# A decoder layer in split float32: gated products and sums on VectorE, a planner that waits for late work, and attention in four groups

## The chip, the cores and the metric

One core of one Trainium2 chip. The time is that of one execution on the device in microseconds (us). The engines are called as in the profile: PE (TensorE, with PEld for its weight loads), DVE (VectorE), ACT (ScalarE), POOL (GpSimd) and SP (SyncE, which issues most of the loads). Lines (L417) are lines of the kernel before, unless the text says after.

## The reference, cut to what matters

One layer for 256 tokens of width 1024 in float32: a pooling mixer and a causal attention with 8 heads of 64 share an input and an output projection; then cross-attention of 4 heads of 256 into 256 memory tokens; then a gated FFN. Each of the three adds its result to a scaled residual and is followed by a layer norm.

```python
z = h @ w_in[l]
u = z[..., :POOL_WIDTH]
q, k, v = ...            # three slices of z, 8 heads of 64 each
pool_out = multiscale_pool(u, w_pool[l], pool_scale[l])
attn_out = moba_attention(q, k, v)          # 256 tokens: one causal block
mix = jnp.concatenate([pool_out, attn_out], axis=-1) @ w_out[l]
h = layer_norm(DEEPNORM_ALPHA * h + mix, ln1_g[l], ln1_b[l])
h = layer_norm(DEEPNORM_ALPHA * h + memory_cross_attention(h, mem, w_xq[l], w_xkv[l], w_xo[l]), ln2_g[l], ln2_b[l])
h = layer_norm(DEEPNORM_ALPHA * h + (jax.nn.silu(h @ w_gate) * (h @ w_up)) @ w_down, ln3_g[l], ln3_b[l])
```

## The kernel before

**Numbers in two parts.** A float32 value is split into two float32r numbers, a high part (ACT casts: w67h from w67r) and a rest (DVE subtracts: w67l). `split` (L473) records the two. A product of two split values is three matmuls, high by high and the two mixed ones (`three`, L465). Scores, attention outputs of the 8 small heads, and transposes are in plain float32. Weights come as pages of 128 x 1024, numbered in order of use: w0 to w16 for q and k, then v, u (from w21 on the memory projections stand beside them), w27 to w34 w_out, w43 to w50 the query projection of the cross-attention, w51 to w58 w_xo, w59 onwards the FFN.

**Who decides the order.** The program first records all its operations in a `Plan` (L138) and then gives each engine a fixed list. PE works in the order in which the code is written. All other engines get their order from a simulation of the whole run: `deadlines` (L190) gives every operation a time by which PE needs it, and `schedule` (L227) lets each engine take, among the operations that are ready by the plan's clock, the one with the earliest deadline. How long an operation takes there is a formula (`cost`, L384). An engine never stands idle for an operation that is not yet ready, if any other is.

**The stages in time.** Projections to q and k; then `do_v`, `do_u` and `do_xk` (the memory keys), generators that PE works off in steps (the code from L871 on). Between their steps stand the small operations of the attention, `scores(hq, t)` (L738: four heads, one tile of 128 queries), `probs_t(hp)` (L766: transposes of the softmax of a pair of heads), `attend(hp)` (L792), and of the pooling, `mix_pool(g)` (its output is the c blocks, c0l for one). After w_out and the first norm comes the cross-attention: `do_xq(h)` for the query projection, with `xscores` (L1047), `xprobs_t` (L1058: transposes of xpr into xst) and `xattend` (L1067: outputs o0 to o3, split into o3h and o3l) between the steps of it and of `project(c_xo, ...)`. `Norm` (L920) does a norm on DVE: `sum` and `measure` for each half of 512 columns, `stats` (with a power on POOL, L945), `centre` and `scale`. In LN2 r20 and r21 are the two tiles of 128 tokens; PE then transposes them into h2T (`ident,r`), which is split too.

**The FFN.** DFF = 2816 in 11 chunks of 256. The first chunk goes by rows of tokens (`rows_of_first`: seven of its eight k steps for tile 0, 21 matmuls, then the first transposes of tile 1). For each of the other ten, `gated` (L1161) adds the two PSUM parts of gate and up on DVE, applies Silu on ACT, and multiplies the two (128 x 512) on POOL. Chunks 1 to 8 multiply with w_down by a seven-product scheme, for which `add_sums` (L1150) forms four sums of the quarters of the gated values, 128 x 128 each, on POOL; the sums of weight quarters come from DRAM for chunks 1 to 6 and are formed on DVE for 7 and 8 (d7, d8). The down phase follows the last chunk, from about 322 us.

Of the kernel before, what the change touches and what calls it, by code (L numbers as in the profile page):

```python
# [18 lines left out]
P = 128  # L19
D = 1024  # L20
S = 256
# [19 lines left out]
class Buf:  # L41
# [11 lines left out]
    @property  # L53
    def grain(self):
        return 512 if self.kind == "bank" else GRAIN
# [72 lines left out]
class Op:  # L128
    __slots__ = ("n", "eng", "fn", "busy", "late", "preds", "succs", "dead", "ready", "wait", "start", "end",
                 "bufs", "locks", "size", "kind", "bias")  # L130
# [4 lines left out]
LEAVE = 2.0  # L135


class Plan:  # L138
# [88 lines left out]
    def schedule(self, room):  # L227
# [10 lines left out]
        free = {"PE": 0.0, "ACT": 0.0, "DVE": 0.0, "POOL": 0.0, "SP": 0.0, "AQ": 0.0}  # L238
        wire = 0.0
        ready = {e: [] for e in free}  # L240
        for o in self.ops:
            o.wait, o.ready = len(o.preds), 0.0
# [4 lines left out]
        dve_lock = 0.0  # L247
        stall = []
# [48 lines left out]
        while len(done) < total:  # L297
            moved = False
            for e in free:
                if free[e] > t:  # L300
                    continue
# [7 lines left out]
                else:  # L309
                    later, tries = [], 0  # L310
                    while ready[e] and tries < 40:
                        item = heappop(ready[e])
                        c = item[2]
                        if c.ready <= t and place(c, t):
                            o = c
                            break
                        later.append(item)
                        tries += 1
# [32 lines left out]
                for s in o.succs:  # L351
# [5 lines left out]
                    s.ready = max(s.ready, at)  # L357
# [4 lines left out]
            nxt = [a for a in free.values() if a > t]  # L362
# [14 lines left out]
class Kit:  # L377


    def __init__(self, nc, plan):  # L380
        self.nc, self.plan = nc, plan
        self.engines = {"ACT": nc.scalar, "DVE": nc.vector, "POOL": nc.gpsimd, "SP": nc.sync, "AQ": nc.scalar}
# [20 lines left out]
    def act(self, out, src, func, bias=0.0, scale=1.0, accum=None, **kw):  # L403
# [7 lines left out]
        busy, late = self.cost("ACT", out.cols)  # L411
        outs = [out] + ([accum] if accum is not None else [])
# [25 lines left out]
    def dma(self, out, src, size, queue="SP", after=(), bias=0.0):  # L438
        q = self.engines[queue]
        val = lambda v: v.ap() if isinstance(v, View) else v  # L440
        return self.plan.op(queue, lambda: q.dma_start(val(out), val(src)), [out], [src], 0.1 if queue == "SP" else 0.4,
                            3.0 + size / 300e3, size=size, after=after, bias=bias)

    def dma_add(self, out, src, size, after=()):
# [3 lines left out]
                            [out], [src], 1.3, 6.0 + size / 100e3, size=2.5 * size, after=after)  # L448
# [38 lines left out]
def decoder_layer(  # L487
    ctx: ExitStack, tc: tile.TileContext, x, x_t, mem_t, w_qkv, w_u, w_pool, w_out,
    ln1_g, ln1_b, w_xq, w_xk, w_xkv, w_xo, ln2_g, ln2_b, w_gu, w_down, w_sum, ln3_g, ln3_b, out,
# [103 lines left out]
    c_qk[0].cut = {0: [(slice(0, 256), "AQ", [slice(0, 128), slice(128, 256)]), (slice(256, 512), "SP", [slice(256, 512)])]}  # L593
# [61 lines left out]
    for _ in range(BUSY):  # L655
        plan.op("PE", lambda: nc.tensor.matmul(ps.ap()[:, :P], spark, spark, start=True, stop=True), [ps], [], 0.22,
# [56 lines left out]


# [23 lines left out]
    def scores(hq, t):  # L738
        w = (t + 1) * P
        pss = [bank(f"ps{j}").re("p (h s) -> p h s", h=2) for j in range(2)]  # L740
        for h in range(2):
            for j in range(2):
# [3 lines left out]
                   0.007 if j == 0 else 2 * w / 2400)  # L746
# [41 lines left out]

    def block_of(name, k):
        return tuple(a[:, 2 * (k % 2):2 * (k % 2) + 2, :].re("p t s -> p (t s)") for a in pair_of(name, k // 2))  # L790

    def attend(hp):  # L792
        s0, s1 = pts[hp]
        po = bank("po")
        for j in range(2):
            hs = slice(j * HD, (j + 1) * HD)
            vs = slice((2 * hp + j) * HD, (2 * hp + j + 1) * HD)
            mm(po[hs, :S], vt[:, 0, vs], s0[:, j, :], True, False, 0.013 if j == 0 else 0.25)
            mm(po[hs, P:S], vt[:, 1, vs], s1[:, j, :], False, True, 0.013 if j == 0 else 0.1)
        split(*block_of("c", 4 + hp), po[:, :S])  # L800
# [19 lines left out]
    def mix_pool(g):  # L820
# [6 lines left out]
        hi, lo = block_of("c", g)  # L827
        act(hi, pm, AF.Copy, 0.0, psc[:, g:g + 1])
        stt(lo, pm, psc[:, g:g + 1], hi.f32, OP.mult, OP.subtract)
# [54 lines left out]
    run(u, 6)  # L884
    scores(1, 1)
# [6 lines left out]
    run(gk, 12)  # L892
    probs_t(2)
    mix_pool(0)
    run(gk, 8)
    probs_t(3)
    mix_pool(1)
    pool_diff(2)
    run(gk, 8)
    attend(2)  # L900
    mix_pool(2)
    pool_diff(3)
    run(gk, 8)
    attend(3)
    mix_pool(3)
    run(gk)

# [93 lines left out]
    mix = project(c_mix, lambda k: block_of("c", k), 4)  # L1001
    norms = []
    for t in range(T):
        norm = Norm(1, t, xt[t])
        for half_ in HALVES:
            norm.add(*half_, until(mix)[1])
        norm.finish()
        norms.append(norm)
    run(mix)
# [16 lines left out]
    gv = do_xv()
    run(gv, 8)
# [418 lines left out]
```

## Time and profile before

| | |
|---|---|
| median of 3 runs | 385.34 us (384.01 to 385.57) |
| the profiled execution, its own time | 385.47 us |
| its span | 383.7 us |
| PE busy | 371.7 us (97% of the span) |
| DVE busy | 286.6 us (75%) |
| ACT busy | 214.7 us (56%) |
| POOL busy | 66.3 us (17%) |
| HBM traffic over the span | 244 GB/s |

Busy time is the union of an engine's instructions; matmuls are pipelined, and their ends are modelled, so PE's pace is read from start to start. In a timeline a row has the start in us, the duration, the engine, the line, the operation, output and inputs with their shapes; "x4" means that four like instructions stand in one row; the bracket at the end is the idle time ahead of it and the instruction that ended it.

### The profile page before, as it was taken

How to read it: one execution, taken by the hardware profiler on the slowest of the kernel's cores; microseconds unless marked ns; L12 is line 12 of the kernel's file. 1: busy time of each engine (PE TensorE's matmuls, PEld its weight loads, DVE VectorE, ACT ScalarE, POOL GpSimd, SP SyncE). 2: the span in 40 equal slices, each digit the busy share in tenths (PEclk: the TensorE clock that was granted, in tenths of full speed). 3: DMA queues.
4: the chain of work that ended last, by engine and by line, in shares of the span. 5: the costliest groups of instructions: out<-in, count | busy, mean ns of one | idle time of the engine just before them, and what ended most of it. 6: DMA issues, size and time to landing. Idle time of an engine off the chain costs nothing.

```text
span 383.7 us, 5499 instructions
## 1 busy us (share of the span) xinstructions
PE 371.7 (97%) x2058; PEld 317.9 (83%) x2058; DVE 286.6 (75%) x384; ACT 214.7 (56%) x324; POOL 66.3 (17%) x73
## 2 busy tenths in 40 slices
PE   8999999999999999899969999999999999999994
PEld 7997878788888898888848888888888888888883
DVE  5889577966599646576898375373866998999994
ACT  5779778643346527458447144452746867677310
POOL 1000027000010000000100073263346440100012
PEclk9999999999999999999998999999999999999999
DMA  7999436376687534538476999998754465999002
GB/s 245 416 417 417 178 111 182 110 252 170 222 287 261 160 114 143 187 113 290 143 289 205 364 381 274 272 278 214 191 181 141 123 188 141 305 386 343 3 2 109
DMA packets 25690, 84.50 MB, mean 220 GB/s; under 512 B 2752, under 2 KB 3520, under 8 KB 25664
## 3 DMA queue, kind: packets, MB, share of 16 engines
q1 hardware_dynamic: 24544, 79.11, 59.0%
q0 software_dynamic: 832, 4.72, 6.6%
q8 instruction: 16, 0.26, 0.3%
q10 hardware_dynamic: 288, 0.33, 0.2%
q14 instruction: 10, 0.08, 0.1%
HBM read 83.10 MB, written 10.49 MB: 244 GB/s over the span
## 4 chain that ended last, share of the span: by engine, by line
PE 72%; issue 14%; DVE 6%; ACT 3%; DMA 3%; POOL 1%; SPq 0%; POOLq 0%; DVEq 0%
PE banks L457 70%; PE banks L462 2%; DMA w7r<-in_w_qkv 2%; DVE r L422 1%; DMA w1r<-in_w_qkv 1%; POOL r L417 1%; ACT xpr L409 1%; POOL sg L417 1%; DVE st L933 0%; DVE w26l L417 0%; DVE w62l L417 0%; DVE w55l L417 0%; ACT pr L409 0%; DVE h2T L417 0%; DVE w57l L417 0%
## 5 line engine op out<-in xcount | busy, mean ns | idle before, releaser
L945 POOL TENSOR_TENSOR rs<-rs,mhalf 128x1 f32<-128x1 f32 x6 | 5.4, 908 | 173.6 <-DVE rs L431 173.6
L417 POOL TENSOR_TENSOR sg<-sg 128x512 f32<-128x512 f32 x10 | 16.7, 1668 | 73.7 <-ACT sg L409 49.2
L417 DVE TENSOR_TENSOR sg<-banks,sg 128x512 f32<-128x512 f32 x20 | 12.8, 682 | 8.4 <-ACT sg L401 8.4
L401 ACT COPY sg<-banks 128x512 f32<-128x512 f32 x20 | 10.7, 587 | 12.4 <-PE banks L457 12.4
L417 POOL TENSOR_TENSOR sums<-sg 128x128 f32<-128x128 f32 x16 | 14.0, 913 | 0.5
L417 POOL TENSOR_TENSOR win<-upad 128x542 f32<-128x542 f32 x2 | 2.2, 1090 | 55.4 <-DVE upad L417 55.4
L422 DVE SCALAR_TENSOR_TENSOR r<-r,mv,g 128x512 f32<-128x512 f32 (+2 forms) x12 | 8.2, 720 | 0.0
L417 POOL TENSOR_TENSOR sums<-sums,sg 128x128 f32<-128x128 f32 x8 | 8.2, 1029 | 0.0
L409 ACT ACTIVATE sg<-sg 128x512 f32<-128x512 f32 x10 | 6.3, 634 | 3.3 <-DVE sg L417 3.3
L401 ACT CAST h2T<-banks 128x512 fp32r<-128x512 f32 x4 | 2.3, 587 | 10.3 <-PE banks L462 10.3
L409 ACT ACTIVATE xpr<-banks,mx 128x256 f32<-128x256 f32 x8 | 3.8, 473 | 7.7 <-DVE mx L732 7.7
L933 DVE BATCH_NORM_STATS2 st<-r 128x6 f32<-128x512 f32 (+1 forms) x12 | 7.9, 665 | 0.2
L732 DVE TENSOR_REDUCE mx<-banks 128x2 f32<-128x512 f32 x4 | 2.8, 691 | 6.9 <-PE banks L457 6.9
L462 PE MATMUL banks<-ident,r 128*128 128x128 f32 x32 | 5.1, 282 | 2.6 <-DVE r L422 2.6
L462 PEld LDWEIGHTS banks<-ident,r 128*128 128x128 f32 x32 | 3.9, 142 | 4.1 <-DVE r L422 3.3
L409 ACT ACTIVATE pr<-pr,mx 128x128 f32<-128x128 f32 (+1 forms) x16 | 7.1, 446 | 0.0
L417 POOL TENSOR_TENSOR sums<-sg,sums 128x128 f32<-128x128 f32 x8 | 6.6, 827 | 0.5
L422 DVE SCALAR_TENSOR_TENSOR r<-r,rs,b 128x512 f32<-128x512 f32 (+1 forms) x10 | 6.6, 703 | 0.1
L755 DVE CUSTOM_DVE_ANT_0 pr<-banks,tri 128x128 f32<-128x128 f32 (+1 forms) x16 | 4.8, 353 | 2.6 <-PE banks L457 2.6
L422 DVE SCALAR_TENSOR_TENSOR xql<-banks,xq 128x512 f32<-128x512 f32 x4 | 2.8, 688 | 5.2 <-ACT xq L409 5.2
L409 ACT ACTIVATE pr<-pr,sm 128x128 f32<-128x128 f32 (+1 forms) x16 | 6.3, 450 | 0.0
L417 DVE TENSOR_TENSOR g2l<-sums,g2h 128x512 fp32r<-128x512 f32 x1 | 0.7, 691 | 7.4 <-ACT g2h L401 7.4
(1096 smaller groups left out, 1302.4 us busy)
## 6 DMA issues: line engine op xcount, KB each, us to landing
sum_z<-in_w_sum SPq DMA_DIRECT2D x2, 1536.0 KB, 11.3
sum_z<-in_w_sum POOLq DMA_DIRECT2D x2, 1536.0 KB, 13.8
y<-in_w_sum SPq DMA_DIRECT2D x6, 512.0 KB, 4.7
z<-sum_z SPq DMA_DIRECT2D x6, 512.0 KB, 4.3
g<-in_ln_g SPq DMA_DIRECT2D x3, 512.0 KB, 5.1
b<-in_ln_b SPq DMA_DIRECT2D x3, 512.0 KB, 5.4
sum_w<-in_w_sum SPq DMA_DIRECT2D x2, 768.0 KB, 12.4
sum_w<-sum_z POOLq DMA_DIRECT2D x2, 768.0 KB, 8.1
```

The lines of the kernel that those rows point to most:

```text
L401: return self.add(eng, lambda: f(out.ap(), src.ap()), out, [src], 1, **kw)
L409: nc.scalar.activation(out.ap(), src.ap(), func, bias=val(bias), scale=val(scale), **more)
L417: return self.add(eng, lambda: e.tensor_tensor(out.ap(), a.ap(), b.ap(), op=op), out, [a, b], 2, **kw)
L422: return self.add(eng, lambda: e.scalar_tensor_tensor(out.ap(), a.ap(), val(scalar), b.ap(), op0=op0, op1=op1), out, [a, b, scalar], 2, **kw)
L457: return self.plan.op("PE", lambda: self.nc.tensor.matmul(ps.ap(), w.ap(), y.ap(), start=start, stop=stop, skip_group_check=True), [ps], [ ...
L462: return self.plan.op("PE", lambda: self.nc.tensor.transpose(ps.ap(), src.ap(), ident.ap()), [ps], [src, ident], 0.109, DRAIN, kind=False)
L732: kit.plan.op("DVE", lambda: nc.vector.tensor_reduce(mx.ap(), src.ap(), op=OP.max, axis=AX.X, negate=True), [mx], [src], *kit.cost("DVE", ...
L755: nc.vector.tensor_tensor_reduce(o.ap(), i.ap(), tri.ap()[:, S - w:], -1.0, -NEG, op0=OP.add, op1=OP.min, accum_out=m.ap())
L933: plan.op("DVE", lambda: nc.vector.bn_stats(st.ap(), r.ap()), [st], [r], *kit.cost("DVE", c1 - c0))
L945: plan.op("POOL", lambda: nc.gpsimd.tensor_tensor(rs.ap(), rs.ap(), mhalf.ap(), op=OP.pow), [rs], [rs, mhalf], 0.83, 0.05)
```

## The change

- **FFN on DVE.** The ten products of `gated` move from POOL to DVE, and so do the sums of `add_sums`, where one 128 x 256 subtraction now forms two of the four: three instructions for a chunk instead of four. POOL keeps the powers of the norms, the pooling windows, its DMAs and LN3's additions. DVE gets 34 instructions more, POOL 42 fewer.
- **The planner holds.** If an operation that is not ready now will be within 0.7 us (`PATIENCE`) and its deadline is less than 1.0 us away, an engine does not start another of more than 0.3 us whose deadline is over 1.5 us later; it waits instead.
- **The plan's durations.** The formulas for DVE, ACT, POOL and the DMA queue have new constants, at most eight loads are in flight by the plan, and DVE's two-input operations are charged for a busy POOL.
- **Attention in four groups.** Two tiles of scores, then the other two with the first two probs_t, then two attend, and so on: where ten float32 groups were divided by float32r steps, there are five.
- **The cross-attention's order** is two tables now. probs_t of head 1 stands six 512-column matmuls later; xattend(3) stands behind six products of o2 instead of ahead of them; the first h2T transposes stand one product (three matmuls) earlier.
- The seven-product code is made general (for w_out, w_xkv and w_xo too), but its tables are empty for these three: the number of matmuls of each shape is as before.

```diff
+PATIENCE = 0.7
...
                     later, tries = [], 0
+                    soon = None
                     while ready[e] and tries < 40:
                         item = heappop(ready[e])
                         c = item[2]
+                        if soon is not None and c.dead > soon + 1.5 and c.busy > 0.3:
+                            later.append(item)
+                            break
                         if c.ready <= t and place(c, t):
                             o = c
                             break
+                        if soon is None and t < c.ready < t + PATIENCE and c.dead < t + 1.0:
+                            soon = c.dead
...
         if eng == "DVE":
-            return (0.035 + n / (1920.0 if fast else 960.0), 0.125)
+            return (0.068 + n / (1900.0 if fast else 958.0), 0.09)
         if eng == "ACT":
-            return (0.14 + n * 0.836e-3, 0.03)
+            return (0.06 + n * 0.865e-3, 0.10)
...
+XQ_STEPS = (23, "s", 0), (13, "p", 0), (3, "s", 1), (15, "p", 1), (4, "s", 2), (4, "a", 0)
+XO_STEPS = (0, "a", 1), (3, "p", 2), (5, "s", 3), (0, "a", 2), (6, "p", 3)
...
+    def add_sums(hl, q):
+
+        a11, a12 = q[:, 0], q[:, 2]
+        more = half("sums", [4, P], hold=10)
+        tt("DVE", more[:, 0:2], q[:, 0:2], q[:, 1:4:2], OP.subtract)
+        tt("DVE", more[:, 2], more[:, 1], a11, OP.subtract)
+        tt("DVE", more[:, 3], a12, more[:, 2], OP.add)
+        split(hl[0], hl[1], more)
...
-    run(v, 2)
+    run(v, 4)
     scores(0, 0)
-    run(v, 4)
     scores(0, 1)
     run(v)
-    run(u, 4)
-    probs_t(0)
     run(u, 6)
     scores(1, 0)
+    scores(1, 1)
+    probs_t(0)
     probs_t(1)
-    run(u, 6)
+    run(u, 14)
     attend(0)
-    run(u, 6)
-    scores(1, 1)
     attend(1)
...
+    xo = xo_rest()
     run(xo, 2)
     xattend(3)
-    last_exp = plan.ops[-1]
+    run(xo, 2)
+    rows_sum(0, 2)
+    run(xo, 4)
+    rows_sum(0, 3)
...
-    run(xo, 3)
-    norm.add(*HALVES[0], acc0)
+    run(xo, 4)
+    rows_sum(1, 4)
+    run(xo, 2)
     transpose_tok(h2T, h2[0], 0, 0)
-    norm.add(*HALVES[1], until(xo)[1])
+    run(xo, 2)
+    rows_sum(1, 0)
...
-        tt("POOL", a, a, b, OP.mult)
+        tt("DVE", a, a, b, OP.mult)
```

Three places in the engines' lists, each before and then after (the lines L4xx of after are those of the same helpers). PE at head 3 of the cross-attention, where w55 to w58 are pages of w_xo, o2 and o3 the outputs of heads 2 and 3, and the products with xst are the last of xattend(3); before:

```order
L457 MATMUL banks_68<-xst_1816,xv1h_1385 128x256 x2
L457 MATMUL banks_68<-xst_1816,xv1l_1390 128x256
L457 MATMUL banks_68<-w55h_1526,o2h_1766 128x512
L457 MATMUL banks_68<-w55l_1556,o2h_1766 128x512
L457 MATMUL banks_68<-w55h_1526,o2l_1776 128x512
L457 MATMUL banks_68<-w56h_1543,o2h_1766 128x512
L457 MATMUL banks_68<-w56l_1570,o2h_1766 128x512
L457 MATMUL banks_68<-w56h_1543,o2l_1776 128x512
L457 MATMUL banks_68<-w57h_1554,o3h_1859 128x512
L457 MATMUL banks_68<-w57l_1581,o3h_1859 128x512
L457 MATMUL banks_68<-w57h_1554,o3l_1871 128x512
```

And after; the six products with w55, w56 and o2 of the first quarter now stand ahead of all the products with xst:

```order
L472 MATMUL banks_68<-xst_1821,xv1h_1385 128x256 x2
L472 MATMUL banks_68<-xst_1821,xv1l_1390 128x256
L472 MATMUL banks_68<-w57h_1589,o3h_1864 128x512
L472 MATMUL banks_68<-w57l_1600,o3h_1864 128x512
L472 MATMUL banks_68<-w57h_1589,o3l_1871 128x512
L472 MATMUL banks_68<-w58h_1597,o3h_1864 128x512
L472 MATMUL banks_68<-w58l_1610,o3h_1864 128x512
L472 MATMUL banks_68<-w58h_1597,o3l_1871 128x512
L472 MATMUL banks_68<-w55h_1514,o2h_1786 128x512
```

The products with o3, which need the result of xattend(3) split in two, stood six matmuls behind it and now stand directly behind it.

DVE in LN2, where r20 and r21 are the two tiles of the norm, g2 and b2 its vectors, st, mv and rs its statistics, h2T0 and h2T1 halves of the transposed tile 0, and w67l to w69l rests of FFN weights; before:

```order
L422 SCALAR_TENSOR_TENSOR r21_1925<-r11_1171,banks_68 128x512
L422 SCALAR_TENSOR_TENSOR r20_1881<-r20_1881,rs_1915,b2_1625 128x512 x2
L933 BN_STATS st_1942<-r21_1925 128x6
L417 TENSOR_TENSOR w67l_1948<-w67r_1831,w67h_1869 128x1024
L417 TENSOR_TENSOR h2T0_1951<-banks_68,h2T0_1951 128x4x128
L422 SCALAR_TENSOR_TENSOR r21_1925<-r11_1171,banks_68 128x512
L417 TENSOR_TENSOR h2T1_1963<-banks_68,h2T1_1963 128x4x128
L933 BN_STATS st_1942<-r21_1925 128x6
L417 TENSOR_TENSOR w68l_1980<-w68r_1837,w68h_1886 128x1024
L943 BN_AGGR mv_1989<-st_1942 128x2
L417 TENSOR_TENSOR w69l_1991<-w69r_1854,w69h_1894 128x1024
L431 TENSOR_SCALAR rs_2000<-mv_1989 128x1
```

And after, from the scaling of r20 on:

```order
L438 SCALAR_TENSOR_TENSOR r20_1883<-r20_1883,rs_1915,b2_1624 128x512
L438 SCALAR_TENSOR_TENSOR r21_1931<-r11_1173,banks_68 128x512
L438 SCALAR_TENSOR_TENSOR r20_1883<-r20_1883,rs_1915,b2_1624 128x512
L433 TENSOR_TENSOR h2T0_1944<-banks_68,h2T0_1944 128x4x128
L1148 BN_STATS st_1955<-r21_1931 128x6
L438 SCALAR_TENSOR_TENSOR r21_1931<-r11_1173,banks_68 128x512
L1148 BN_STATS st_1955<-r21_1931 128x6
L433 TENSOR_TENSOR h2T1_1962<-banks_68,h2T1_1962 128x4x128
L1158 BN_AGGR mv_1978<-st_1955 128x2
L447 TENSOR_SCALAR rs_1981<-mv_1978 128x1
L438 SCALAR_TENSOR_TENSOR r21_1931<-r21_1931,mv_1978,g2_1616 128x512 x2
L438 SCALAR_TENSOR_TENSOR r21_1931<-r21_1931,rs_1981,b2_1624 128x512 x2
```

One half of r20's scaling now comes ahead of r21's sum, and the weight splits w67l, w68l, w69l (and w70l, which came right behind these rows) have left the chain of r21: all of them come behind its scaling.

DVE in the FFN at chunk 2, where sg are gate and up of the chunk, sums the four sums for the seven products and g2l the rest of the split; before (POOL had the product and the sums):

```order
L417 TENSOR_TENSOR w82l_2257<-w82r_2120,w82h_2241 128x1024
L417 TENSOR_TENSOR sg_2279<-banks_68,sg_2279 128x512
L417 TENSOR_TENSOR sg_2285<-banks_68,sg_2285 128x512
L417 TENSOR_TENSOR g2l_2317<-sg_2279,g2h_2311 128x512
L417 TENSOR_TENSOR w83l_2323<-w83r_2175,w83h_2255 128x1024
```

And after:

```order
L433 TENSOR_TENSOR sg_2278<-banks_68,sg_2278 128x512
L433 TENSOR_TENSOR sg_2284<-banks_68,sg_2284 128x512
L433 TENSOR_TENSOR sg_2278<-sg_2278,sg_2284 128x512
L433 TENSOR_TENSOR sums_2304<-sg_2278 128x256
L433 TENSOR_TENSOR sums_2304<-sums_2304,sg_2278 128x128
L433 TENSOR_TENSOR sums_2304<-sg_2278,sums_2304 128x128
L433 TENSOR_TENSOR g2l_2318<-sg_2278,g2h_2307 128x512
L433 TENSOR_TENSOR g2l_2318<-sums_2304,g2h_2307 128x512
L433 TENSOR_TENSOR w83l_2333<-w83r_2171,w83h_2242 128x1024
```

A product and three sums stand between the two PSUM additions and the split, and w83l has moved behind them.

More of the change, by code (lines that the diff above doesn't have):

```diff
@@ L237, in schedule @@
         taken = {k: [] for k in room}
-        free = {"PE": 0.0, "ACT": 0.0, "DVE": 0.0, "POOL": 0.0, "SP": 0.0, "AQ": 0.0}
+        free = {"PE": 0.0, "ACT": 0.0, "DVE": 0.5, "POOL": 2.0, "SP": 0.0}
+        landed = []
         wire = 0.0
@@ new lines, in decoder_layer, with __init__, into, seven @@
+    class Blocks:
+        def __init__(self, name):
+            self.name, self.m, self.begun = name, {}, set()
+        def into(self, n, y, w, cols=ALL):
+            if n not in self.m:
+                self.m[n] = bank(f"{self.name}{n}")
+            three(self.m[n][:, cols], y, w, n not in self.begun, True)
+            self.begun.add(n)
+        def seven(self, form, weights, order):
+            for n, f, what in order:
+                self.into(n, form(f), weights.get(what))
+                yield
+        def eight(self, form, weights, k0, ns=(2, 3, 4, 0)):
+            for k in range(2):
+                for n in ns:
+                    t, c0, c1 = QUARTERS[n]
+                    self.into(n, form(2 * k + t), pair(weights.get(k0 + k), ALL, slice(c0, c1)))
+                    yield
+        def joined(self):
+            m1, u2, u3 = [half(f"{self.name}{u}", [512], hold=12) for u in ("m1", "u2", "u3")]
+            copy("ACT", m1, self.m[1])
+            tt("DVE", u2, self.m[6], m1, OP.add)
+            tt("DVE", u3, self.m[7], u2, OP.add)
+            return m1, u2, u3
@@ new lines, in decoder_layer, with xo_head @@
+    xqs = (step for g in xq for step in g)
+    for n, what, h in XQ_STEPS:
+        run(xqs, n)
+        small[what](h)
+    run(xqs)
+    h2T = Both("h2T")
+    xo_sums, xo_order = sums_of("xo", s_xo, XO)
+    if xo_sums:
+        xo_sums.begin(slice(0, xo_sums.n), [marks['xv']])
+        xo_sums.add(slice(0, xo_sums.n))
+    xb = Blocks("xo")
+    def xo_head():
+        for h in range(2):
+            if XO[h]:
+                yield from xb.seven(form_of("o", h), weights_of(XO[h], f"xo{h}", c_xo, h, xo_sums, xo_order),
+                                    ORDER_S if XO[h] == "S" else ORDER)
+            else:
+                yield from xb.eight(form_of("o", h), c_xo, 2 * h)
@@ new lines, in xo_rest, with rows_sum @@
+    def xo_rest():
+        for n in (2, 3, 4, 0):
+            for h in (2, 3):
+                yield from xb.eight(form_of("o", h), c_xo, 2 * h, (n,))
+    norms = [Norm(2, t, h1[t]) for t in range(T)]
+    h2 = [norm.r for norm in norms]
+    def rows_sum(t, n):
+        c0, c1 = QUARTERS[n][1:]
+        if any(XO):
+            with_acc(norms[t], c0, c1, xb.m[n])
+        else:
+            norms[t].sum(c0, c1, xb.m[n])
+        norms[t].measure(c0, c1)
+    xo = xo_head()
+    for n, what, h in XO_STEPS:
+        run(xo, n)
+        small[what](h)
@@ L1345, in decoder_layer @@
     for half_ in HALVES:
-        add(norm, *half_, until(dn))
+        with_acc(norm, *half_, until(dn))
     for half_ in HALVES:
@@ L1375, in decoder_layer @@
     copy("ACT", norm.r[:, CUT:], ps_end)
[L1376 removed]
+    store(1, norm.r, CUT, D, "ACT")
     norm.scale(512, CUT)
```

491 lines of the change are left out of this document (287 added, 204 removed).

## The prediction

> **What bounds the kernel now.** I read first where TensorE is not busy, since the whole run is 97% TensorE. The windows view of before gives, for a stretch, its length and then the busy time of PE, PEld, DVE, ACT and POOL, the granted clock, the DMA share and GB/s.
>
> ```profile
> 185.00:205.00 20.00, 16.65 (x74) 13.02 (x73) 19.01 (x29) 9.54 (x13) 1.91 (x2) 0.93 0.60 211
> 205.00:322.00 117.00, 117.00 (x665) 102.39 (x664) 78.81 (x79) 59.52 (x82) 45.73 (x45) 1.00 0.78 232
> 322.00:360.00 38.00, 38.00 (x169) 31.48 (x168) 36.85 (x40) 28.25 (x32) 1.99 (x1) 1.00 0.79 282
> ```
>
> The FFN (205 to 360) is PE without a hole; an edit there gains nothing and can only lose. LN2 (185 to 205) has 3.35 us of idle PE and a clock below full. The PE waits, largest first among those that the change touches (total, times, longest):
>
> ```profile
> PE banks L462 <- DVE r L422: 2.6, 1, 2.6
> PE banks L462 <- ACT xpr L409: 1.1, 1, 1.1
> PE banks L457 <- DVE h2T L417: 0.7, 1, 0.7
> ```
>
> So the sum below has a term for LN2, one for the first softmax of the cross-attention, and one for the attention; for each I look at what ends the wait, and whether the new order moves it.
>
> **Attention in four groups.** The float32 score and value products stand between float32r products. PE rows of before (start, time, instruction):
>
> ```profile
> 52.34 0.63 PE L457 MATMUL banks<-xT,w17l 128*128 128x256 f32 x4
> 52.91 1.13 PE L457 MATMUL banks<-kT,qT 64*128 64x256 f32 x8
> 53.97 0.88 PE L457 MATMUL banks<-sb,vt 128*64 128x256 f32 x8
> 54.78 0.74 PE L457 MATMUL banks<-xT,w17l 128*128 128x256 f32 x4
> 55.36 0.86 PE L457 MATMUL banks<-xT,w18h 128*128 128x512 f32 x3
> ...
> 66.68 0.38 PE L462 MATMUL banks<-ident,pr 128*128 128x128 f32 x2
> 67.29 0.55 PE L462 MATMUL banks<-ident,pr 128*128 128x128 f32 x3 [0.24 <-DVE c0l L422]
> ```
>
> Four 256-column products at 0.12 are 0.48; the start of the first row to the next group is 0.57, and from 54.78 to 55.36 is 0.58. A group therefore costs about 0.09 going in and 0.10 coming out. The ten such groups become five, as the order shows: five times 0.19 is 0.95. The transposes at 66.68 stop for 0.39 (0.61 from row to row, two transposes are 0.22) for c0l, a split of the pooling product; in the new order both transposes come ahead of it. Together **-1.3**. It can be -2.0, or -0.5 if two of these boundaries come back as waits, because scores(0,1) and scores(1,1) are now asked for sooner behind their k and q splits and probs_t(1) sooner behind its softmax.
>
> **First softmax of the cross-attention.** The PE rows, and then the pieces of the chain of waits there:
>
> ```profile
> 151.83 1.55 PE L457 MATMUL banks<-h1T,w49h 128*128 128x512 f32 x6
> 154.43 0.94 PE L462 MATMUL banks<-ident,xpr 128*128 128x128 f32 x4 [1.05 <-ACT xpr L409]
> 155.13 0.71 PE L457 MATMUL banks<-h1T,w49h 128*128 128x512 f32 x2
> ```
>
> ```profile
> 151.49 1.13 DVE w56l L417
> 152.62 1.14 DVE w57l L417
> 153.87 0.92 ACT xpr L409 x2
> ```
>
> PE is through with the six products at 151.83 + 6 x 0.227 = 153.19, starts the transposes at 154.43 and takes 0.70 for what four transposes of 0.109 do in 0.44: 1.24 + 0.26 = 1.50 lost. The wait ends with the softmax's scaling, and that stood behind three weight splits on DVE. The change does two things: the transposes stand six 512-column products later (1.36 us, so PE comes at 154.55), and DVE has one split (1.13) less ahead of the reciprocal, so the scaling is done by 153.2 rather than 154.3. Either alone nearly covers it: **-1.5** (at least -0.8, if only one holds and the transposes keep their 0.26).
>
> **Head 3 and w_xo, a wait that is added.** PE, ACT and DVE in order of time:
>
> ```profile
> 180.10 0.28 PE L457 MATMUL banks<-xst,xv1l 128*128 128x256 f32 x1
> 180.22 0.40 PE L457 MATMUL banks<-w55h,o2h 128*128 128x512 f32 x1
> 180.42 0.59 ACT L401 CAST o3h<-banks 128x512 fp32r<-128x512 f32 x1 [0.54 <-PE banks L457]
> 181.10 0.68 DVE L417 TENSOR_TENSOR o3l<-banks,o3h 128x512 fp32r<-128x512 f32 x1
> ...
> 181.98 1.28 ACT L1114 ACT_TABLE_LOAD   x1
> ```
>
> Call X = 180.22 the end of xattend(3). ACT casts o3h from X+0.20 to X+0.79; DVE has o3l at X+1.56. Before, six products with o2 (1.36) filled this time. They now stand ahead of xattend(3), and the first product with o3h stands right behind it: it starts at X+0.85, and the one with o3l at X+1.62 instead of X+0.45. That is **+1.2**. The bounds are 0.8 (the cast comes at once and PE waits for DVE alone) and 1.7 (the table load, which the new ACT order puts ahead of the cast, ends late or DVE is inside a 1.13 us split). Queued behind the wait on PE is all the rest, but the work behind this point on DVE (LN2) moves with it, so the price is paid once.
>
> **LN2.** DVE, PE and POOL in order of time:
>
> ```profile
> 188.98 0.68 DVE L422 SCALAR_TENSOR_TENSOR r<-r,banks 128x512 f32<-128x512 f32 x1
> 189.58 1.41 DVE L422 SCALAR_TENSOR_TENSOR r<-r,rs,b 128x512 f32<-128x512 f32 x2
> 189.77 0.39 PE L457 MATMUL banks<-w57h,o3h 128*128 128x512 f32 x1
> 190.46 0.60 PE L462 MATMUL banks<-ident,r 128*128 128x128 f32 x4
> ...
> 193.37 0.74 PE L457 MATMUL banks<-w59h,h2T 128*128 128x512 f32 x2 [0.71 <-DVE h2T L417]
> ...
> 197.65 0.92 POOL L945 TENSOR_TENSOR rs<-rs,mhalf 128x1 f32<-128x1 f32 x1 [8.84 <-DVE rs L431]
> 198.75 1.21 DVE L417 TENSOR_TENSOR w70l<-w70r,w70h 128x1024 fp32r<-128x1024 f32 x1
> 200.68 0.66 PE L462 MATMUL banks<-ident,r 128*128 128x128 f32 x4 [2.63 <-DVE r L422]
> 202.34 0.78 PE L457 MATMUL banks<-w59h,h2T 128*128 128x512 f32 x1
> 202.91 0.63 PE L457 MATMUL banks<-w59l,h2T 128*128 128x512 f32 x1
> ...
> 205.74 0.63 PE L457 MATMUL banks<-w60h,h2T 128*128 128x512 f32 x2
> ```
>
> Four splits (w67l to w70l) stand inside the chain of the norm's second half, at 1.13 each 4.5 us. After, all four stand behind it. My timetable, in before's clock: the lower half of r20 is scaled from 188.98 instead of 189.58; PE, whose transposes now stand three products earlier, starts them at about 189.86, does four (0.44), six products (1.36) and four transposes (0.44), and begins t=0's FFN rows at 192.10. From there 21 products of 0.23 bring it to the next transposes at 196.9. DVE needs, from 188.98, eleven steps of 512 columns (188.98 to 189.58 is 0.60; I allow up to 0.65), 0.2 until h2T's cast is there, and 0.2 for the two tiny ones; POOL's 0.92 lies beside the centring. The lower half of r21 is there between 196.0 and 196.6, ahead of PE. Four transposes, three products, four transposes: t=1's rows start at 198.6 instead of 202.34, **-3.7**. Before, those rows also ran slow: from 202.34 to 205.74 eight products took 3.40, at 0.43 each, where full pace is 8 x 0.23 = 1.84. Without the wait of 2.63 the clock has no reason to fall: **-1.6**. Together **-5.3**, at least -4.0 if a wait of about 1.3 stays.
>
> On the clock, the Trainium skill (TensorE: Matmul & The Clock Gate, Part 1: The HAM clock gate) says that an idle window of about 3.4 us halves it; the trace's 2.63 us wait was enough here, and the 1.05 us one at 154 was not.
>
> **FFN: products and sums on DVE.** A page line of before (busy, mean ns), then rows of DVE, POOL and PE:
>
> ```profile
> L417 POOL TENSOR_TENSOR sg<-sg 128x512 f32<-128x512 f32 x10 | 16.7, 1668 | 73.7 <-ACT sg L409 49.2
> ```
>
> ```profile
> 303.00 2.15 POOL L417 TENSOR_TENSOR sg<-sg 128x512 f32<-128x512 f32 x1 [6.47 <-ACT sg L409]
> 303.91 2.33 DVE L417 TENSOR_TENSOR y1l<-y,y1h 128x1024 fp32r<-128x1024 f32 x1
> ...
> 357.23 1.22 DVE L417 TENSOR_TENSOR d8l<-d8x,d8h 128x1024 fp32r<-128x1024 f32 x1
> 358.70 0.39 PE L457 MATMUL banks<-d8l,g8h 128*128 128x512 f32 x1
> ```
>
> DVE gets ten products of 0.60, and eight times a 256-column and two 128-column subtractions. A 512-column step is 0.60 and a 1024-column one 1.13, so by the straight line 256 columns are about 0.34 and 128 about 0.20 (an estimate): 6.0 + 8 x 0.74 = +12.0. Against it, DVE no longer collides with POOL: y1l took 2.33 beside a POOL product instead of 1.22 for the same shape. I allow 5 to 11 us for that over the FFN, so DVE there is 78.8 + 12.0 less 5 to 11, 80 to 86 of 117: it keeps over 30 us free, which is the cover. Where there is no cover is the down phase, 36.85 of 38.00 busy; its tightest row is d8l, ready at 358.45 and used at 358.70. There the new order adds 1.7 us (a split and a product) ahead of it, but takes w104l (1.13) away from before it and frees it of POOL's collision; the net is about half a microsecond less. **0** (-0.3 to +2).
>
> On moving work between these two engines the Trainium skill (Perfetto Trace Analysis, Optimizing Scalar/DVE Operations) says both that a saturated DVE may be relieved by GpSimd and that the two share an SBUF read port, so that it might not help; the first speaks against this change in the down phase, and y1l's 2.33 speaks for the second.
>
> **The sum.** -1.3 - 1.5 + 1.2 - 5.3 + 0 = -6.9. The traced execution was 385.47 (span 383.7 and 1.8 around it), 0.13 above the median 385.34 of the runs shown; so 378.6 in its terms, **378.4** as a median.
>
> **The rivals.** *DVE becomes the bound* (4%, slower): if the 12.0 us are not relieved and the planner lets DVE run late into the down phase, d8l comes 12.0 - 0.25 = 11.7 late and PE, with no slack behind it, waits as long: 378.4 + 11.7 = 390.1. It decides against the change once DVE is more than 7.2 us (6.9 + 0.25) late at d8l. For it: 36.85 of 38.00. Against: 38 us of idle DVE ahead of 322, and only one POOL instruction (1.99) of the 45.73 us lies behind. *LN2 stays half open* (12%): if the centring of r21 or POOL's 0.92 us ends about 1.3 late, PE still stands there, and the clock still closes: the gain there is 2.5 instead of 5.3, 381.2. For it: margins of only 0.3 to 0.9 in my timetable. *The merged attention groups wait* (8%): scores and softmax are asked for earlier, and a softmax that isn't ready costs what the cross-attention's first one lost, 1.5; two of them give 378.4 + 3.0 = 381.4. For it: kT and probs_t(1) have less work ahead of them. Against: the splits that were late (c0l) were late through the old order. *Nothing comes of it* (6%): DMA sets the pace (share 0.78 of all engines in the FFN), and what PE wins up to 205 it waits for behind w-loads: about 385. Against it: PE has not a single hole from 205 to 360 now.
>
> **The numbers.** The forecast has 70%. The range is **376.0 to 382.0**: below, the better ends of the attention (-0.5), the new wait (-0.4), LN2's and FFN's (-0.6) with some more; above, the half-open LN2 and the slower groups. What is left out are DVE as the bound, no gain, and some mishaps together. Within 0.5% (383.4 to 387.3, about what a measurement of this kernel can tell from no change) lies the no-gain case: 0.06; slower 0.04; faster 0.90.
>
> **What would show it.** After: PE waits for r and xpr gone, a new PE wait of 0.8 and some 0.3 for o3h and o3l at L472, 185 to 205 with a clock of 1.00, FFN still without holes, DVE at about 80 to 86 in the same stretch, 512-column POOL products gone. It is wrong if PE waits in the down phase for d-splits or sums, if `r` still heads the PE waits, or if kT or pr heads them in the attention.

## The result, and the profile after

The changed kernel takes 378.75 us (median of 4 runs, 378.01 to 379.30) against 385.45 (384.01 to 385.64) for the kernel before beside it: a ratio of 0.9837 (95% interval 0.9815 to 0.9858), 6.7 us less. 378.4 was forecast. The profiled execution took 378.92, with a span of 376.8 (383.7 before).

The windows view of after, for the three stretches shown of before (all now stand some 2 to 7 us earlier): LN2, the FFN's chunks, the down phase. Its columns are as there.

```profile
183.00:198.00 15.00, 15.00 (x75) 12.06 (x73) 13.41 (x24) 7.21 (x10) 1.91 (x2) 1.00 0.67 245
198.00:315.00 117.00, 117.00 (x668) 103.19 (x668) 87.51 (x117) 61.42 (x84) 3.97 (x4) 1.00 0.78 241
315.00:353.00 38.00, 38.00 (x169) 31.45 (x168) 36.20 (x41) 28.46 (x32) 0.00 (x0) 1.00 0.74 270
```

LN2 has no idle PE left and a granted clock of 1.00; POOL has gone from 45.73 to 3.97 in the chunks, DVE from 78.81 to 87.51, and PE still has no hole there. The PE waits of after that the change has to do with:

```profile
PE banks L472 <- ACT o3h L415: 0.7, 1, 0.7
PE banks L477 <- DVE mx L780: 0.5, 1, 0.5
PE banks L472 <- DVE r L438: 0.4, 1, 0.4
```

The waits for r (2.6), xpr (1.1) and h2T (0.7) of before are gone. Three have come in their place: o3h, which was forecast; mx at the second probs_t; and another r, at the first norm.

Where the time went is read from when PE starts the same product in both traces. The last column adds up to the change of the span.

| PE's first product with | before | after | shift | gained since the row above |
|---|---|---|---|---|
| w11 (scores begin) | 28.76 | 28.79 | +0.02 | +0.02 |
| w25 (attention over) | 80.46 | 79.43 | -1.02 | -1.04 |
| w47 (behind w_out, first norm) | 144.20 | 143.91 | -0.28 | +0.74 |
| w51 (query projection over) | 163.68 | 161.72 | -1.96 | -1.68 |
| w57 with o3h | 181.61 | 180.13 | -1.48 | +0.48 |
| w63 (LN2 and first chunk over) | 209.46 | 203.06 | -6.39 | -4.92 |
| g1 (down phase begins) | 321.74 | 314.79 | -6.95 | -0.56 |
| end of the span | 383.68 | 376.77 | -6.91 | +0.04 |

Two rows hold gains that the list of waits does not show, since each is a short stop inside a group of transposes. Those of xpr for head 0 take 0.55 before and 0.35 after (in the row to w51), those for head 3 take 0.70 and 0.35 (in the row to w57): before, PE came to them while the second half of their softmax was still being scaled.

**Attention.** PE and DVE at the transposes of the first two pairs of heads, in after:

```profile
44.97 1.23 DVE L433 TENSOR_TENSOR w23l<-w23r,w23h 128x1024 fp32r<-128x1024 f32 x1 [0.49 <-ACT w23h L415]
45.31 0.87 PE L477 MATMUL banks<-ident,pr 128*128 128x128 f32 x6
46.11 0.28 DVE L780 CUSTOM_DVE_ANT_0 pr<-banks,tri 128x128 f32<-128x128 f32 x1
46.32 0.29 DVE L780 CUSTOM_DVE_ANT_0 pr<-banks,tri 128x128 f32<-128x128 f32 x1
46.67 1.08 PE L477 MATMUL banks<-ident,pr 128*128 128x128 f32 x6 [0.48 <-DVE mx L780]
```

Six transposes of 0.109 end at 45.96, the next six start at 46.67: a hole of 0.7 that was not there before. The softmax that they transpose was scaled on ACT by 41.14, so they do not wait for it. They wait for DVE to read the new scores out of their PSUM bank (L780), and DVE comes to that only behind the weight split w23l.

**First softmax of the cross-attention** (as the prediction calls it; it is head 1's). PE and ACT in after:

```profile
151.39 2.00 PE L472 MATMUL banks<-h1T,w49h 128*128 128x512 f32 x8
152.09 0.90 ACT L423 ACTIVATE xpr<-xpr,sm 128x256 f32<-128x256 f32 x2
...
154.15 0.60 PE L477 MATMUL banks<-ident,xpr 128*128 128x128 f32 x4
```

The scaling ends at 152.99, PE comes at 154.15: over a microsecond of slack where before it waited 1.24.

**Head 3.** PE, ACT and DVE in after:

```profile
179.17 0.28 PE L472 MATMUL banks<-xst,xv1l 128*128 128x256 f32 x1
179.49 0.58 ACT L415 CAST o3h<-banks 128x512 fp32r<-128x512 f32 x1 [0.20 <-PE banks L472]
...
180.11 0.69 DVE L433 TENSOR_TENSOR o3l<-banks,o3h 128x512 fp32r<-128x512 f32 x1
180.13 0.50 PE L472 MATMUL banks<-w57h,o3h 128*128 128x512 f32 x1 [0.68 <-ACT o3h L415]
...
180.85 0.50 PE L472 MATMUL banks<-w57h,o3l 128*128 128x512 f32 x1
```

xattend(3) ends at X = 179.17 + 0.12 = 179.29; the product with o3h starts at X+0.84 and the one with o3l at X+1.56.

**LN2.** DVE, PE and POOL in after:

```profile
187.89 0.75 DVE L438 SCALAR_TENSOR_TENSOR r<-r,rs,b 128x512 f32<-128x512 f32 x1
188.56 0.68 DVE L438 SCALAR_TENSOR_TENSOR r<-r,banks 128x512 f32<-128x512 f32 x1
188.69 0.66 PE L477 MATMUL banks<-ident,r 128*128 128x128 f32 x4
...
190.93 0.48 PE L472 MATMUL banks<-w59h,h2T 128*128 128x512 f32 x1
...
194.75 1.40 DVE L438 SCALAR_TENSOR_TENSOR r<-r,rs,b 128x512 f32<-128x512 f32 x2
...
195.82 0.60 PE L477 MATMUL banks<-ident,r 128*128 128x128 f32 x4
196.07 1.21 DVE L433 TENSOR_TENSOR w67l<-w67r,w67h 128x1024 fp32r<-128x1024 f32 x1
...
197.33 0.48 PE L472 MATMUL banks<-w59h,h2T 128*128 128x512 f32 x1
```

From the first transposes to the FFN rows PE takes 190.93 - 188.69 = 2.24, from there to the next transposes 4.89. The lower half of r21 is scaled at 194.75 + 0.70 = 195.45, 0.37 ahead of PE. The first split behind it, w67l, starts at 196.07.

### The profile page after: what moved, and what is told of

Read it like the earlier page. It is cut to its first block, busy times and chain, and to the rows that moved or that the text cites. A ratio compares the mean times of both kernels' runs of the same rounds, so it can differ in the third digit from the quotient of the medians.

```text
span 376.8 us, 5461 instructions
## 1 busy us (share of the span) xinstructions
PE 368.9 (98%) x2058; PEld 318.4 (85%) x2058; DVE 288.6 (77%) x418; ACT 214.8 (57%) x324; POOL 21.4 (6%) x31
## 5 line engine op out<-in xcount | busy, mean ns | idle before, releaser
L433 DVE TENSOR_TENSOR xst<-banks,xst 128x512 fp32r<-128x512 f32 x4 | 2.8, 690 | 6.1 <-ACT xst L415 6.1
L433 DVE TENSOR_TENSOR sg<-sg 128x512 f32<-128x512 f32 x10 | 6.8, 685 | 0.2
L433 POOL TENSOR_TENSOR win<-upad 128x542 f32<-128x542 f32 x2 | 3.1, 1542 | 55.5 <-DVE upad L433 55.5
L415 ACT CAST h1T<-banks 128x512 fp32r<-128x512 f32 x4 | 2.4, 588 | 6.3 <-PE banks L477 6.3
L423 ACT ACTIVATE pr<-pr,sm 128x256 f32<-128x256 f32 (+1 forms) x16 | 5.8, 442 | 0.0
L433 DVE TENSOR_TENSOR w40l<-w40r,w40h 128x1024 fp32r<-128x1024 f32 x1 | 1.2, 1224 | 5.2 <-ACT w40h L415 5.2
L438 DVE SCALAR_TENSOR_TENSOR r<-r,banks 128x512 f32<-128x512 f32 x6 | 4.0, 680 | 1.5 <-PE banks L472 1.5
L423 ACT ACTIVATE xq<-banks 128x512 fp32r<-128x512 f32 x4 | 2.4, 596 | 4.6 <-PE banks L472 4.6
L433 DVE TENSOR_TENSOR h1T<-banks,h1T 128x512 fp32r<-128x512 f32 x4 | 2.7, 686 | 2.9 <-ACT h1T L415 2.9
```

The costliest lines, as they stand in the source:

```text
L415: return self.add(eng, lambda: f(out.ap(), src.ap()), out, [src], 1, **kw)
L423: nc.scalar.activation(out.ap(), src.ap(), func, bias=val(bias), scale=val(scale), **more)
L433: return self.add(eng, lambda: e.tensor_tensor(out.ap(), a.ap(), b.ap(), op=op), out, [a, b], 2, **kw)
L438: return self.add(eng, lambda: e.scalar_tensor_tensor(out.ap(), a.ap(), val(scalar), b.ap(), op0=op0, op1=op1), out, [a, b, scalar], 2, **kw)
```

## The experiments

Each time stands beside runs of the kernel before on the same chip, whose median was 384.60 to 385.45; so ratios compare better than times from one experiment to the next. Four runs asked which part of the change makes the gain.

**Products and sums back on POOL**, in the changed kernel:

```diff
-        tt("DVE", a, a, b, OP.mult)
+        tt("POOL", a, a, b, OP.mult)
...
-        tt("DVE", more[:, 0:2], q[:, 0:2], q[:, 1:4:2], OP.subtract)
-        tt("DVE", more[:, 2], more[:, 1], a11, OP.subtract)
-        tt("DVE", more[:, 3], a12, more[:, 2], OP.add)
+        tt("POOL", more[:, 0:2], q[:, 0:2], q[:, 1:4:2], OP.subtract)
+        tt("POOL", more[:, 2], more[:, 1], a11, OP.subtract)
+        tt("POOL", more[:, 3], a12, more[:, 2], OP.add)
```

> The changed kernel with the ten gated products and the three sums a chunk back on POOL; all that stands ahead of the FFN is in the same order as in the changed kernel. Theory (the FFN move is worth about nothing, the gain lies ahead of it): 378.8, at most 0.7 more, with LN2, the cross-attention and the attention as in the changed kernel; if POOL at work makes PE's FFN steps slower, a chunk takes 11.18 as before and not 11.11, +0.6 in all. Rival (the product on DVE carries the gain, since DVE no longer collides with POOL): 381 or more, with PE waits in the FFN.

378.85; ratio to before 0.9855 (0.9832 to 0.9877), the changed kernel's was 0.9837. The difference is not clear of noise. The windows row of its chunks:

```profile
198.00:315.00 117.00, 116.81 (x667) 102.60 (x666) 81.59 (x83) 59.47 (x82) 44.64 (x37) 1.00 0.75 237
```

DVE is busy for 81.59 instead of 87.51. In this stretch of the changed kernel the moved operations (33 of the 34) take DVE 13.3 us, counted from the start of each to the next start or to its own end; they add only 5.9, so about 7.4 us of its time beside POOL were collisions. The 35 weight splits alone take 45.2 here and 40.3 there.

PE's time from w63 to g1 is 112.32, 0.59 more than in the changed kernel. All of that stands at w79 and w80, where PE waits for DVE to empty a PSUM bank, and DVE comes to it only behind three weight splits (w84l to w86l):

```profile
247.16 1.27 DVE L433 TENSOR_TENSOR sg<-banks,sg 128x512 f32<-128x512 f32 x2
247.89 2.25 PE L472 MATMUL banks<-h2T,w79h 128*128 128x512 f32 x8 [0.19 <-DVE sg L433]
```

So in the changed kernel the move may be worth 0.6; one profile alone shows it. Elsewhere PE's chunks keep the changed kernel's pace (11.11 from w83 to w87) with POOL at work, so POOL isn't what sets that.

**The same move alone, in the kernel before:**

```diff
-        tt("POOL", a, a, b, OP.mult)
+        tt("DVE", a, a, b, OP.mult)
...
-        tt("POOL", s1, a21, a22, OP.subtract)
-        tt("POOL", s3, a11, a21, OP.subtract)
-        tt("POOL", s2, s1, a11, OP.subtract)
-        tt("POOL", s4, a12, s2, OP.add)
+        tt("DVE", s1, a21, a22, OP.subtract)
+        tt("DVE", s3, a11, a21, OP.subtract)
+        tt("DVE", s2, s1, a11, OP.subtract)
+        tt("DVE", s4, a12, s2, OP.add)
```

> The kernel before with only one thing changed: the ten gated products and the four sums a chunk are on DVE. All ahead of the FFN is as before. Theory: 385.4, or up to 0.6 less if PE's chunk goes from 11.18 to 11.11 once POOL is quiet; no PE wait in the FFN. Rival (DVE becomes the bound in the down phase, as the prediction's slower case has it): over 387, with PE waiting for d8l. Rival (collisions): under 383.5.

385.46; ratio 1.0015 (0.9998 to 1.0031): in the kernel before, the move changes nothing. PE's chunk stays at 11.18 with POOL quiet.

**The hold alone, in the kernel before:**

```diff
+PATIENCE = 0.7
...
+                    soon = None
...
+                        if soon is not None and c.dead > soon + 1.5 and c.busy > 0.3:
+                            later.append(item)
+                            break
...
+                        if soon is None and t < c.ready < t + PATIENCE and c.dead < t + 1.0:
+                            soon = c.dead
```

> The kernel before with only the planner's hold (0.7 us) added; durations, groups and PE's order as before. In LN2 three of the four weight splits (w68l, w69l, w70l) leave the chain of r21; w67l stays. Theory: 3 x 1.13 = 3.4 off the chain ends the wait of 2.63, and with it the clock's fall (1.6); the wait of 0.71 for h2T stays: 385.4 - 4.3 = 381.1. Rival (the hold does little by itself, it is the new durations and PE's three earlier products that do it): less than 2 gained, 383.5 or more.

379.56; ratio 0.9871 (0.9851 to 0.9892). More than expected, and not from LN2: that gave 4.29 (the product with w57 and o3h is 1.96 earlier than before, w63 6.25), as worked out. The rest is the c0l wait, gone (0.44 gained between w13 and w25), the first softmax of the cross-attention (1.07 gained between w47 and w51) and the transposes of head 3 (0.34 between w51 and w57), which the hold freed too, with PE's steps where they were. LN2 in this run:

```profile
191.41 0.73 PE L464 MATMUL banks<-w59h,h2T 128*128 128x512 f32 x2 [0.71 <-DVE h2T L424]
...
194.82 1.41 DVE L429 SCALAR_TENSOR_TENSOR r<-r,rs,b 128x512 f32<-128x512 f32 x2
195.92 0.60 PE L469 MATMUL banks<-ident,r 128*128 128x128 f32 x4
```

The wait for h2T is still there, since w67l still stands ahead of it; the one for r is gone, with r ready at 195.52 and PE there at 195.92.

**No hold, in the changed kernel** (`PATIENCE = 0.0`):

> The changed kernel with the planner's hold at zero. In LN2 three splits (w67l, w68l, w69l) come back into the chain of r21, 3.4 us. Theory: the lower half of r21 is scaled 3.4 later, PE waits about 2.5 for it, the clock falls and costs 1.6 more: 378.8 + 4.1 = 382.9. Rival (PE's earlier transposes and the new durations carry LN2's gain): under 380.5, clock at 1.00 in LN2.

381.88; ratio 0.9931 (0.9906 to 0.9956). 3.1 lost, not 4.1 (by the profile 3.2, from w57 to w63). PE in LN2, and the window over it:

```profile
194.33 0.73 PE L472 MATMUL banks<-w61h,h2T 128*128 128x512 f32 x2 [0.81 <-DVE h2T L433]
...
197.59 0.66 PE L477 MATMUL banks<-ident,r 128*128 128x128 f32 x4 [1.37 <-DVE r L438]
```

```profile
183.00:203.00 20.00, 17.68 (x83) 13.65 (x83) 18.97 (x29) 9.48 (x12) 1.97 (x2) 1.00 0.50 184
```

The splits back in the chain do make PE wait, twice, but the wait for r is 1.37 and not 2.5, because the one for h2T (0.81) has already held PE back; and the clock stays at 1.00. Between w47 and w51 nothing is lost (17.84; 17.81 in the changed kernel, 19.48 before): there PE's later transposes suffice by themselves, since the scaling ends at 152.82 and PE comes at 152.97; 1.36 earlier it would have waited.

**More on DVE.** How far is DVE from being the bound? In the changed kernel, two and then five more operations behind each product that leave its value as it is:

```diff
         tt("DVE", a, a, b, OP.mult)
+        for _ in range(2):
+            tt("DVE", a, a, a, OP.max)
```

> The changed kernel with two more DVE operations of 128 x 512 behind each gated product (a maximum of the value with itself, in place, so on the way to the split): 20 x 0.60 = 12 us more DVE in the FFN, as much again as the change has added. Theory (DVE has 30 us free there): 378.8, at most 0.5 more. Rival (DVE is at its bound after the change): +5 to +12, with PE waits in the FFN or the down phase.

> As the run with 12 us more, but five such operations behind each product: 50 x 0.60 = 30 us, as much as DVE has free in the FFN by the changed kernel's windows (117.00 less 87.51). Theory: DVE is full now and PE waits, above all in the down phase where DVE had no slack: between +3 and +12, 382 to 391. Rival (the down phase is fed ahead, so that the free time is more than it looks): under 380.

380.64 and 388.44; ratios 0.9870 (0.9841 to 0.9899) and 1.0072 (1.0047 to 1.0096). In neither does the chunks' part lose anything: g1 starts at 314.72 and 314.38 (314.79 in the changed kernel). With five, the down phase does: from g1 to w103 it takes 44.64 instead of 38.10. Its window (DVE is the fourth figure) and its PE waits:

```profile
315.00:353.00 38.00, 35.41 (x149) 26.90 (x148) 37.78 (x45) 29.23 (x33) 0.00 (x0) 1.00 0.76 270
```

```profile
PE banks L472 <- ACT diag L423: 2.8, 1, 2.8
...
PE banks L472 <- DVE d8l L433: 0.8, 1, 0.8
PE banks L472 <- DVE d4wl L433: 0.8, 1, 0.8
...
PE banks L472 <- DVE d7l L433: 0.6, 1, 0.6
PE banks L472 <- DVE d3wl L433: 0.6, 1, 0.6
```

This is the slower rival in its place: DVE enters the down phase late and PE waits there for the splits. With two, my 0.5 was too little: the down phase loses 0.24, but the last norm loses 1.7, which both runs show. The last wait of PE, after and then with two:

```profile
371.92 0.91 PE L472 MATMUL banks<-r,diag 128*128 128x384 f32 x2 [1.40 <-ACT diag L423]
```

```profile
374.03 0.91 PE L472 MATMUL banks<-r,diag 128*128 128x384 f32 x2 [2.79 <-ACT diag L423]
```

The planner has put the first tile's centring between the second tile's sums there, so POOL's addition for the first tile (371.73 to 372.99) now stands ahead of the power that diag needs: that starts at 372.95 instead of 370.88. Whether a later DVE or the other plan alone does that was not separated.

**The ten groups of before, in the changed kernel:**

```diff
-    run(v, 4)
+    run(v, 2)
     scores(0, 0)
+    run(v, 4)
     scores(0, 1)
...
```

> The changed kernel with the attention in the ten groups of before. Theory (boundaries cost 0.19 each, the c0l wait 0.4, and the new groups brought a wait of 0.6 for a PSUM bank at the second probs_t): 378.8 + 0.95 + 0.4 - 0.6 = 379.5, if the new plan leaves c0l as late as before, 379.1 if not. Rival (the four groups are what moved the time): 381 or more.

380.06; ratio 0.9852 (0.9831 to 0.9873): 1.3 more than the changed kernel by the medians, 0.6 by the ratios, and by another way than expected. With the scores earlier, PE meets a kT that the new plan casts later:

```profile
31.05 0.71 PE L472 MATMUL banks<-kT,qT 64*128 64x128 f32 x8 [1.16 <-ACT kT L415]
```

From w11 to w25 this kernel takes 52.42, some 1.2 of it this wait, and the run with scores(1,1) later (below), which has five groups and neither wait, takes 50.08: so the five boundaries are worth about 1.1, near the 0.95 worked out. The changed kernel takes 50.64, so half of that was paid back at the second probs_t. The wait for c0l is absent in both, so it was not the groups that removed it.

**Where the new waits can go.** First the o3 wait, with the six o2 products of the second quarter behind xattend(3):

```diff
-        for n in (2, 3, 4, 0):
-            for h in (2, 3):
-                yield from xb.eight(form_of("o", h), c_xo, 2 * h, (n,))
+        for n, h in ((2, 2), (3, 2), (2, 3), (3, 3), (4, 2), (4, 3), (0, 2), (0, 3)):
+            yield from xb.eight(form_of("o", h), c_xo, 2 * h, (n,))
...
     run(xo, 2)
     xattend(3)
-    run(xo, 2)
+    run(xo, 4)
     rows_sum(0, 2)
-    run(xo, 4)
+    run(xo, 2)
     rows_sum(0, 3)
```

> The changed kernel with the last products of w_xo in another order: the six products of o2 for the second quarter now stand between xattend(3) and the first product with o3, so that eighteen o1 and o2 products stand around it as cover. Theory (the wait at o3 is a plain hole of 1.2 us that any work behind xattend(3) fills): o3 wait gone, 378.8 - 1.2 = 377.6, LN2 as in the changed kernel. Rival (the first half of r20 is summed six products later, and LN2 gives it back): 378.5 or more with a PE wait for r.

377.50; ratio 0.9787 (0.9765 to 0.9809). The wait is gone:

```profile
178.13 0.59 ACT L415 CAST o3h<-banks 128x512 fp32r<-128x512 f32 x1 [0.21 <-PE banks L472]
...
178.75 0.69 DVE L433 TENSOR_TENSOR o3l<-banks,o3h 128x512 fp32r<-128x512 f32 x1
...
179.32 0.39 PE L472 MATMUL banks<-w57h,o3h 128*128 128x512 f32 x1
...
179.78 0.39 PE L472 MATMUL banks<-w57h,o3l 128*128 128x512 f32 x1
```

From w55 to w63, with the same work in it, PE takes 25.40 (175.12 to 200.52) instead of 26.58 (176.48 to 203.06): 1.18, the forecast price of the wait.

Then the changed kernel again, and beside it scores(1,1) moved to the third group (same number of groups, two PSUM banks fewer at the second probs_t), and both covers together. In the third the first norm's sums also have a bias of 3.0 in the plan, whose own effect was not separated.

```diff
     scores(1, 0)
-    scores(1, 1)
     probs_t(0)
     probs_t(1)
     run(u, 14)
+    scores(1, 1)
     attend(0)
```

> The changed kernel once more, as the base for the two runs beside it: 378.8, within 0.7. The wait of 0.54 at the first norm (PE for the bank that r11's sum frees) came, by theory, from one late landing (w40r at 98.60, while the runs with the same order up to there had it between 96.1 and 97.1) and is absent here; a rival, that the new order of DVE always has it, expects it again.

> The changed kernel with scores(1,1) moved from the second attention group to the third, so that still five groups stand there, but no more than eight PSUM banks are asked for at the second probs_t. Theory (the new wait of 0.4 to 1.0 at the second probs_t is for a bank that the scores hold): that wait is gone, 0.6 to 0.7 less than the changed kernel beside it. Rival (it waits for the softmax itself): the wait stays, or comes back at the third group; no gain.

> The changed kernel with scores(1,1) in the third group, the o2 products of the second quarter behind xattend(3), and the sums of the first norm given an earlier deadline by 3 us in the plan. Theory: the gains add, -1.2 for o3 and -0.6 for the bank, 1.8 less than the changed kernel beside it, 377.0; faster than both kernels. Rival (one of them is given back in the down phase, where d8l waited 0.4 in the run with o2 alone): 377.5 or more.

378.69, 377.67 and 376.80; ratios 0.9834 (0.9811 to 0.9856), 0.9812 (0.9793 to 0.9831) and 0.9783 (0.9760 to 0.9805). In the changed kernel again the wait of 0.4 at the first norm is absent: from w31 to w35 PE takes 10.88, as before, and not 11.43. Of the runs with DVE's order the same up to there only the profiled one of after has it, where w40r landed 2.5 behind PE's start on w31 (98.60 and 96.09; 0.8 to 1.8 in four others): w40l stands ahead of r10's sum, and a late landing holds both. With scores(1,1) later the twelve transposes run through, so the wait was for a bank that the scores held:

```profile
44.23 1.53 PE L477 MATMUL banks<-ident,pr 128*128 128x128 f32 x12
```

(The gain of 1.0 by the medians is more than the bank's: from w11 to w25 it is 0.99, of which 0.5 is a wait for kT that the changed kernel beside it happened to have.) With both, the medians add to 1.9 (1.8 expected), and this one is the lowest of all, though its interval overlaps that of the run with o2 alone. What stops it from more is where the slower rival looked: w103 is 8.65 earlier than before, g1 9.22, because DVE has one more split (w104l) ahead of d8l at the end of the down phase; it begins at 347.51, 0.3 before ACT has d8h ready for d8l. DVE and PE of that run:

```profile
348.65 1.22 DVE L433 TENSOR_TENSOR d8l<-d8x,d8h 128x1024 fp32r<-128x1024 f32 x1
```

```profile
349.92 0.50 PE L472 MATMUL banks<-d8l,g8h 128*128 128x512 f32 x1 [0.27 <-DVE d8l L433]
```

## Why the prediction was right, point by point

The sum was right (378.4; 378.75 measured), and three of its five terms hit their size. That the total came within 0.4 is partly luck, since misses cancel: in the profiled execution the attention gained 0.3 less than worked out and the first norm lost 0.7 that no term had, while the FFN gained 0.6 and the transposes of heads 0 and 3 gained 0.5, which no term had either.

- **LN2, -5.3.** Right. The table's -4.92 from w57 to w63 holds 0.38 of the o3l wait, which falls behind the first product with o3h; less that it is 5.3. The timetable held step by step: 2.24 and 4.89 where 2.24 and 4.8 were worked out, and a margin of 0.37 where 0.3 to 0.9 was. The hold is what does it: alone it gives 4.3, and without it the changed kernel loses 3.1. PE's earlier transposes and the h2T split ahead of w67l come with the last microsecond; the plan's new durations were not run alone, so their share in this is open. The clock's 1.6 was a term of before only; with 0.81 and 1.37 of wait in the run without the hold it isn't paid.
- **First softmax, -1.5.** Right (-1.68 to w51, 0.2 of it head 0's transposes). The 154.3 for the end of the scaling was misread, though: its row ends at 154.79. That either half would do is shown on both sides: the hold alone gains 1.07 there, the later transposes alone (no hold) 1.64.
- **Head 3, +1.2.** Right, and the mechanism shown: X+0.84 and X+1.56 against X+0.85 and X+1.62, and 1.18 comes back when other products cover it. The table shows less (0.48, and 0.38 behind the first product with o3h), since 0.34 was gained at head 3's transposes in the same stretch.
- **Attention, -1.3.** Mis-sized: -1.04 in the profiled execution, and that is its better end. From w11 to w25 the changed kernel's order takes 50.64 to 51.21 in six runs, and before's 51.69 and 51.70 in two, so the gain is 0.5 to 1.0; the waits for kT and at the second probs_t come and go. From w25 to w31 the new groups take 16.66 in every run instead of 16.49. The step "five times 0.19" was right (1.1) but counted what leaves and not what comes in: the groups ask for more PSUM banks at once than the kernel's eight, and PE stands 0.7 at the second probs_t (waits of 0.3 to 1.0 in other runs). The text had that place, but blamed a softmax; that was ready 5 us ahead, and the run with scores(1,1) later shows the bank. The c0l part of the term (0.4) was right in size and wrong in cause: the hold removes it, with the old groups.
- **FFN, 0.** Right within its range (-0.3 to +2) as to the product and the sums: alone they change nothing, and beside the rest of the change they spare at most the 0.59 of one wait. The moved operations cost more than worked out (13.3, not 12.0), and DVE's relief of 7.4 lay within the 5 to 11. DVE's 87.51 is over the 80 to 86, since splits that left LN2 are done in this stretch: with POOL at work again it is still 81.59 against 78.81 before. The margin at d8l grew from 0.25 to 0.53. But the chunks gained 0.56 that no step had: PE's pace, below.
- **The rivals.** DVE as the bound did not come, and the runs say how far off it was: 12 us more leave the FFN whole and 30 us more bring the waits in the down phase. It is the next bound, as the last run's d8l shows. The half-open LN2 is what the changed kernel would have been without the hold. No gain from DMA pace: the FFN's chunks start 6.4 to 7 us earlier throughout.

## What to carry to other kernels

When a planner fills an idle engine greedily, look for long work that stands in a short chain by a hair: one rule (hold 0.7 us for what is due) alone brings 5.0 of the change's 6.7 us, and the moved arithmetic alone nothing. The new wait at the second probs_t and the late d8l of the last run are of the same kind: a split of 1.1 us just ahead of what PE needed. Count what a regrouping takes (PSUM banks, the cover behind a result that must be split) as carefully as the boundaries it saves; a result that needs two engines' work before its use wants as much work behind it as that takes (here 1.56 us). And where PE had no hole, more work on a half-idle engine was free up to the stage in which that engine has no slack: here the down phase and the last norm.

## What the runs showed of the hardware

- Two waits of PE, 0.81 and 1.37, with 3.3 us between their ends, left the granted clock at 1.00; before, 0.71 and 2.63 with 7.3 us between brought eight products at 0.43. The Trainium skill (TensorE: Matmul & The Clock Gate, Part 1: The HAM clock gate) gives an idle window of about 3.4 us for the fall; no run here has one that long among PE's products, and 2.63 sufficed. The clock fell behind that wait, not in it (1.00 from 200 to 202, 0.53 from 202 to 204).
- POOL's 40 us of arithmetic in the FFN cost DVE about 7.4 us of collisions, so work moved off POOL costs DVE a little under half its price (5.9 of 13.3). The Trainium skill (Perfetto Trace Analysis, Optimizing Scalar/DVE Operations) says that moving work between the two might not help; here it did not change the time beyond noise, as DVE was not the bound.
- In the kernel before, and in it with the hold or with the product on DVE, 512-column products of two or three of the four pages of a chunk start some 0.234 apart and 11.18 us go to a chunk; in the changed kernel 0.227 and 11.11. POOL is not the cause (quiet and 11.18 in one run, at work and 11.11 in another). It is worth 0.56 us from w63 to g1, and its cause is open.
- PE's time of arrival at w9, with the same code up to there, spreads over 0.8 us (22.32 to 23.15) between runs, and a wait for kT of 0.5 right behind it comes and goes. Terms under half a microsecond in the first 30 us can't be told from that by one profile.
